# Layer 0's input projection in a two-layer encoder: three float32r passes in place of exact fp32 products, and another order in the last piece

## The chip, the core and the metric

The kernel runs on one core of one Trainium2 chip. The metric is the device time of one execution in microseconds; the time before is the median of three runs. Names of engines: PE (TensorE, the matrix engine), with its weight loads listed apart; DVE (VectorE); ACT (ScalarE); POOL (GpSimd); SP (SyncE, which issues the transfers). Results of matmuls are collected in PSUM, in eight banks of 128 x 512 fp32; six of them are "acc" tiles here and two serve everything else.

## What is computed

The reference is a trunk of two encoder layers on 256 positions of width 2048, in float32. Cut to what matters here:

```python
c_act = jax.nn.silu(c)
for l in range(2):
    mod = (c_act @ w_mod[l] + b_mod[l]).reshape(1, 6, 2048)
    shift_m, scale_m, gate_m, shift_f, scale_f, gate_f = ...
    h = layer_norm(x) * (1.0 + scale_m) + shift_m
    proj = h @ w_in[l]                       # 2048 x 4288
    uv, q_c, kv_c, k_r, sb, sc, sh, ag = jnp.split(proj, IN_SPLITS, axis=-1)
    y_a = gmlp_mixer(uv, ...)                # gelu, layer norm of v, mixing over positions
    y_b = mla_mixer(q_c, kv_c, k_r, ...)     # attention with latent q and kv
    y_c = sb * causal_dwconv(sc * sh, sconv_w[l])
    y_d = conformer_conv(ag, ...)            # a * sigmoid(g), conv of 31 taps, norm, silu
    y = concat([y_a, y_b, y_c, y_d]) @ w_out[l]
    x = layer_norm(ALPHA * x + (1.0 + gate_m) * y, ...)
    h = layer_norm(x) * (1.0 + scale_f) + shift_f
    x = layer_norm(ALPHA * x + (1.0 + gate_f) * conv_ffn(h, ...), ...)
```

Each weight is read once, some 600 MB in all.

## The kernel before

**Two ways to multiply.** A product of fp32 operands can be made exactly, as one matmul call on fp32 tiles (the trace shows it as two matmul records), or in three float32r passes: each operand is taken apart into a rounded high half and the remainder, and high x high, high x low and low x high are added in PSUM. The function `weights` (L420) loads a weight tile for either. With `exact` it loads straight into buffers of the pool `splitp` (tags whi and wlo, four tiles of 128 x 1024 each), which the products read as they are. Otherwise it loads into one of the four raw buffers of 128 x 2048 (`rawp`), ACT casts the high half into a whi tile (L455), and DVE subtracts it from the raw tile to get the low half, wlo (L456). `split` (L472) does the same to activations (L474, L475).

**Groups of columns.** The 4288 columns of w_in are handled as D (the GLU pair, 1024 columns), U and V (512 each, for the gMLP branch), E (512, the gate of the short convolution), B (q, kv and the rotary key: 704, read as 768) and C (1024). A unit of a group is `nk` k tiles of 128 rows. `group` (L477) makes such a group over all sixteen k tiles: `load(u)` calls `weights`, `products` issues the matmuls, `end` calls what follows. With `hF` given, all its units are exact. `stream` (L399) issues one unit: the load, the products of the unit before, `pump()` (which takes steps of the modulation stream at a rate set for each phase), and up to `bg` items from the list `background`.

**Layer 0 by pieces.** In layer 0 the normalised input must wait for shift and scale, which are themselves products with w_mod. So `by_pieces` (L1174) goes over the k tiles in five pieces of 2, 2, 4, 4 and 4 (`PIECES`), and while one piece is multiplied, the modulation columns of the next are made: `mod_piece` loads w_mod and DVE multiplies and adds it into `qacc` (L235), PE sums over partitions (`ps_mod`), and the next piece's activations are scaled and, from the fifth k tile on (`PLAIN_KT = 4`), split into halves in `hT`. Within a piece the D group comes in quarters, and U, V and E stand between them: D, U, D, V, D, E, D. `chan_major` issues the products of D, U and E (channels on partitions, 256 positions moving), and V is made with positions on partitions (512 channels moving). D adds up in four PSUM tiles through all pieces. U, V and E use two at a time; `side` adds each piece's result to a sum in SBUF. In the first two pieces all is exact. In the other three the D group passes in halves, while U, V and E are exact:

```python
for j, p in enumerate(weights(w_in, kt, nk, c0, width, exact or g != "D")):
```

`terms` returns one product or three, by whether the weight part has a low half.

**What follows.** After the last piece come `mix_d` (sigmoid and product of the GLU pair; it then puts the 4 x 31 taps of the convolution and `norm_d` into `background`, one item each; the first tap of each of four channel blocks runs on ACT, the other thirty on DVE, L834), `mix_u`, `gelu_v` and `mix_v` (the gMLP branch), then the B group with seven background items a unit and 1.3 modulation steps a unit, the C group with eight and 1.6 (`STEPS`, `RATES`), and the output projection in three column chunks, the first in halves and the other two exact. The modulation stream (`mod_stream`) makes the rows or columns of the remaining five modulations of layer 0 and of layer 1, sixteen loads of 1 MB and sixteen DVE steps into `macc` (L235) for each; the loads use the same four raw buffers. The second half of the positions of the last chunk of the output projection stands behind the sums of shift_f and scale_f (`before` in `out_proj`), which are among the first three modulations of the stream.

**Order.** The program text gives each instruction its place in a priority order; the engines' queues are then filled by a scheduler that takes what it holds to be ready, so the trace's order need not be that of the text. Each engine, and SP's queue of loads, executes its own instructions in order.

Of the kernel before, what the change touches and what calls it, by code (L numbers as in the profile page):

```python
# [14 lines left out]
D = 2048  # L15
# [3 lines left out]
KT = D // P  # L19
# [6 lines left out]
C_UV, C_Q, C_SB, C_SC, C_AG = 0, 1024, 1728, 2240, 3264  # L26
# [13 lines left out]
STEPS = [  # L40
    dict(B=7, C=8, up=2),
    dict(U=6, B=5, C=6, E=6, up=2),
]

PIECES = ((0, 2), (2, 2), (4, 4), (8, 4), (12, 4))

PLAIN_KT = 4


@with_exitstack  # L50
def encoder_kernel(ctx: ExitStack, tc: tile.TileContext, A: dict, consts: bass.AP, out: bass.AP):
# [337 lines left out]
    background = []  # L389
# [84 lines left out]
        act.copy(hi, src)  # L474
        dve.tensor_tensor(out=lo, in0=src, in1=hi.bitcast(F32), op=ALU.subtract)  # L475

    def group(w, c0, width, name, then, ntm=0, nk=2, hF=None, bg=0, spare=0):  # L477

        ncm = (width - 512 * ntm) // P
        box = {}

        def products(item, u):
            if u == 0:
                box["c"] = [acc_tile(f"{name}_c{i}") for i in range((ncm + 1) // 2)]
                box["t"] = [[acc_tile(f"{name}_t{t}{i}") for i in range(ntm)] for t in range(2)]
                box["h"] = list(hT)
            for part in (range(0, min(4, ncm)), range(4, ncm)):
                for k, (hi, lo) in enumerate(item):  # L490
                    kt = u * nk + k
                    st, sp = kt == 0, kt == KT - 1
                    for i in part:
                        o = box["c"][i // 2][:, (i % 2) * S : (i % 2 + 1) * S]
                        off = slice(i * P, (i + 1) * P)
                        first = st and i % 2 == 0
                        if lo is None:
                            mm(o, hi[:, off], hF(kt), first, sp)
                        else:
                            xh, xl = (h[:, kt % 2, :] for h in box["h"][kt // 2][:2])  # L500
                            mm(o, hi[:, off], xh, first, False)
                            mm(o, hi[:, off], xl, False, False)
                            mm(o, lo[:, off], xh, False, sp)
            for k, (hi, lo) in enumerate(item):
                kt = u * nk + k
                st, sp = kt == 0, kt == KT - 1
                for i in range(ntm):
                    off = slice(ncm * P + i * 512, ncm * P + (i + 1) * 512)
                    for t in range(2):
                        tok = slice(t * P, (t + 1) * P)  # L510
                        o = box["t"][t][i]
                        if lo is None:
                            mm(o, hF(kt)[:, tok], hi[:, off], st, sp)
                        else:
                            xh, xl = (h[:, kt % 2, tok] for h in box["h"][kt // 2][:2])
                            mm(o, xh, hi[:, off], st, False)
                            mm(o, xh, lo[:, off], False, False)
                            mm(o, xl, hi[:, off], False, sp)

        def load(u, spare=spare):  # L520
            return weights(w, u * nk, nk, c0, width, hF is not None, spare if u == 0 else 0)

        def end():
            then(box["c"], box["t"])

        return KT // nk, load, products, end, bg
# [52 lines left out]
    def run(g):  # L579
        units, load, products, end, bg = g  # L580
        for u in range(units):
            stream(lambda: load(u), lambda item, u=u: products(item, u), bg)
        pending.append(end)
# [590 lines left out]
    def by_pieces(l, w_in, hF, between, mix_d, mix_u, gelu_v, mix_v, mix_b, mix_c, mix_e):  # L1174
# [27 lines left out]
        def side(g, parts, k0, nkt):  # L1202
            ps = [acc_tile(f"{g}{l}_{i}") for i in range(2)]
            for kt, part in parts:
                st, sp = kt == k0, kt == k0 + nkt - 1
                if g == "V":
                    ts = terms(kt, part)
                    for t in range(2):
                        for n, (w, x) in enumerate(ts):
                            mm(ps[t], x[:, t * P : (t + 1) * P], w, st and n == 0, sp and n == len(ts) - 1)  # L1210
                else:
                    chan_major(ps, kt, part, range(4), st, sp)
            for i in range(2):
                if k0 == 0:
                    act.copy(sums[g][i], ps[i])
                elif k0 + nkt == KT:
                    dve.tensor_tensor(out=sums[g][i], in0=ps[i], in1=sums[g][i], op=ALU.add)
                else:
                    part = tmp_tile("part")
                    act.copy(part, ps[i])  # L1220
                    dve.tensor_tensor(out=sums[g][i], in0=part, in1=sums[g][i], op=ALU.add)
# [3 lines left out]
        for q, (k0, nkt) in enumerate(PIECES):  # L1225
            ahead = between(q + 1) if q + 1 < len(PIECES) else ([], None)
            exact = k0 < PLAIN_KT
            loaded = {}

            def load(g, kt):  # L1230

                c0, width = (C_AG, 1024) if g == "D" else (cols[g], 512)
                nk = min(2048 // width, nkt)
                for j, p in enumerate(weights(w_in, kt, nk, c0, width, exact or g != "D")):
                    loaded[(g, kt + j)] = p

            mods_left = list(ahead[0])
            units = len(mods_left)

            def some_mods(share):  # L1240
                while mods_left and (units - len(mods_left)) < units * share:
                    mods_left.pop(0)()

            def d_part(kt, half):
                if ("D", kt) not in loaded:
                    load("D", kt)
                chan_major(accD, kt, loaded[("D", kt)], range(4 * half, 4 * half + 4), kt == 0, kt == KT - 1)

            turns_d = [(kt, h) for kt in range(k0, k0 + nkt) for h in range(2)]
            n = len(turns_d) // 4  # L1250
            for s in range(4):
                mine = turns_d[s * n : (s + 1) * n]
                if ("D", mine[0][0]) not in loaded:
                    load("D", mine[0][0])
                some_mods((0.3, 0.7, 1.0, 1.0)[s])
                if s == 3 and ahead[1] is not None:
                    ahead[1]()
                for kt, h in mine:
                    d_part(kt, h)
                if s < 3:  # L1260
                    g = "UVE"[s]
                    load(g, k0)
                    some_mods((0.5, 0.85, 1.0)[s])
                    side(g, [(kt, loaded[(g, kt)]) for kt in range(k0, k0 + nkt)], k0, nkt)
        mix_d(accD, None)
        mix_u(sums["U"], None)
        for t in range(2):
            gelu_v(t, sums["V"][t])
        mix_v()
        phase(l, "B")  # L1270
        run(group(w_in, C_Q, 768, f"B{l}", mix_b, hF=hf, bg=STEPS[l]["B"]))
        phase(l, "C")

        def mix_ce(cps, tps):
# [260 lines left out]
```

## Time and profile before

| what | value |
|---|---|
| median of three runs | 2287.88 us (2284.08 to 2291.81) |
| the profiled execution, its own time | 2285.5 us |
| its span | 2283.7 us |
| mean granted PE clock | 0.991 |
| bytes moved | 605.21 MB, mean 265 GB/s |
| layer 0's input projection, first matmul to the end of C | 33 to 325 us |
| its five pieces end at about | 51, 79, 119, 155 and 190 us |

In a row of a view by groups stand the source line, engine, operation, the tiles written and read, their shapes and the count; then busy us and the mean ns of one; then the idle time of the engine just before, and what ended it. L79 is the helper that issues matmuls, so products are told apart by tile names: `hF` and `wexact` are exact operands, `whi`, `wlo` and `hT` are halves. In a row of the order of time stand the start, the length, and what ran, merged where equal instructions follow each other. A matmul's length there includes its way through the array, so rates are taken from starts. Stretches of the span are given as start:end in us from the span's start.

### The profile page before, as it was taken

What the parts mean: (1) busy time and instruction counts of PE and PEld (TensorE: products, weight loads), DVE (VectorE), ACT (ScalarE), POOL (GpSimd) and SP (SyncE); (2) the same over time, 40 slices, a digit from 0 to 9 for tenths busy, and PEclk for the clock granted to TensorE, in tenths of its full rate; (3) what the DMA queues carried; (4) which work ended last, traced back from release to release, by engine and by line L of the source; (5) the groups of instructions that cost most, each with busy time, mean ns of one, the idle gap of its engine ahead of it and who ended that gap; (6) DMA issues with size and microseconds to landing.
All of it is one profiled execution on the core that took longest, in us unless ns stands there. A gap on an engine that the chain in (4) does not pass through costs nothing. (4 is left out here: it accounts for less than half of the span.)

```text
span 2283.7 us, 30024 instructions
## 1 busy us (share of the span) xinstructions
PE 2226.7 (98%) x11682; PEld 1859.8 (81%) x11682; DVE 1788.8 (78%) x2270; ACT 1049.8 (46%) x1525; POOL 35.3 (2%) x59
## 2 busy tenths in 40 slices
PE   5899999999999999999999999999999999999998
PEld 4688886478888888887887999877888888888886
DVE  6878998598888898998976799787776565665676
ACT  2221141355554544544556434556555554454553
POOL 2000000000000000000000000000000000000000
PEclk9999999999999999999999999999999999999999
DMA  9999889778998988888974666876765556555554
GB/s 348 368 335 342 304 301 393 301 267 304 319 329 302 323 312 327 317 316 304 319 258 148 200 214 240 291 268 223 247 223 190 184 182 199 186 196 190 193 194 147
DMA packets 224566, 605.21 MB, mean 265 GB/s; under 512 B 14548, under 2 KB 27076, under 8 KB 202660
## 3 DMA queue, kind: packets, MB, share of 16 engines
q1 hardware_dynamic: 223576, 602.30, 74.7%
q8 instruction: 91, 1.49, 0.3%
q0 software_dynamic: 848, 1.01, 0.1%
q14 instruction: 51, 0.42, 0.0%
HBM read 601.16 MB, written 2.10 MB: 264 GB/s over the span
## 5 line engine op out<-in xcount | busy, mean ns | idle before, releaser
L456 DVE TENSOR_TENSOR wlo<-wraw,whi 128x1024 fp32r<-128x1024 f32 (+1 forms) x624 | 749.6, 1214 | 315.5 <-ACT whi L455 309.4
L455 ACT CAST whi<-wraw 128x1024 fp32r<-128x1024 f32 (+1 forms) x624 | 649.2, 1047 | 727.2 <-PE g_c L79 204.4
L79 PE MATMUL v_c<-hT,whi 128*128 128x512 f32 x1408 | 493.1, 394 | 0.0
L79 PE MATMUL g_c<-hT,whi 128*128 128x512 f32 x1280 | 448.2, 394 | 0.0
L79 PE MATMUL v_c<-hT,wlo 128*128 128x256 f32 x1408 | 394.3, 280 | 0.0
L79 PE MATMUL d<-whi,a 128*128 128x512 f32 x1344 | 387.9, 390 | 0.0
L235 DVE SCALAR_TENSOR_TENSOR macc<-wmod,cact,macc 128x2048 f32<-128x2048 f32 x150 | 351.6, 2344 | 17.1 <-DMA wmod<-in_w_mod_dram 16.8
L79 PE MATMUL g_c<-hT,wlo 128*128 128x256 f32 x1280 | 358.4, 280 | 0.0
L79 PEld LDWEIGHTS v_c<-hT,whi 128*128 128x128 f32 x1408 | 263.9, 187 | 61.0
L79 PEld LDWEIGHTS d<-whi,a 128*128 128x128 f32 x1344 | 252.9, 188 | 52.4
L79 PEld LDWEIGHTS g_c<-hT,whi 128*128 128x128 f32 x1280 | 239.9, 187 | 55.6
L79 PEld LDWEIGHTS v_c<-hT,wlo 128*128 128x128 f32 x1408 | 265.8, 189 | 0.2
L79 PEld LDWEIGHTS g_c<-hT,wlo 128*128 128x128 f32 x1280 | 241.7, 189 | 0.2
L79 PE MATMUL d<-wlo,a 128*128 128x512 f32 x672 | 233.8, 390 | 1.9 <-DVE wlo L456 1.9
L79 PEld LDWEIGHTS d<-wlo,a 128*128 128x128 f32 x672 | 126.6, 188 | 29.1 <-DVE wlo L456 2.7
L79 PE MATMUL o<-whi,a 128*128 128x512 f32 x352 | 102.3, 398 | 2.3 <-ACT whi L455 2.3
L834 DVE SCALAR_TENSOR_TENSOR convD<-gluD,pm,convD 128x237 f32<-128x237 f32 (+26 forms) x240 | 99.0, 458 | 0.5
L474 ACT CAST a<-g 128x512 fp32r<-128x512 f32 x132 | 81.1, 616 | 36.7 <-PE d L79 34.2
L79 PE MATMUL D_c<-hT,whi 128*128 128x256 f32 x448 | 85.7, 292 | 4.0 <-ACT hT L474 3.0
L475 DVE TENSOR_TENSOR a<-g,a 128x512 fp32r<-128x512 f32 x132 | 87.5, 683 | 1.8 <-ACT a L474 1.8
L566 PE MATMUL first<-wexact,hN 128*128 128x512 f32 x192 | 85.7, 596 | 1.5 <-ACT hN L82 1.2
L235 DVE SCALAR_TENSOR_TENSOR qacc<-wmod,cact,qacc 128x1024 f32<-128x1024 f32 (+1 forms) x75 | 80.2, 1070 | 2.4 <-DMA wmod<-in_w_mod_dram 0.4
(311 smaller groups left out, 2462.3 us busy)
## 6 DMA issues: line engine op xcount, KB each, us to landing
wraw<-in_ffn_w_up_dram SPq DMA_DIRECT2D x168, 1024.0 KB, 5.2
wmod<-in_w_mod_dram SPq DMA_DIRECT2D x160, 1024.0 KB, 6.6
wraw<-in_ffn_w_down_dram SPq DMA_DIRECT2D x88, 1024.0 KB, 5.3
wmod<-in_w_mod_dram SPq DMA_DIRECT2D x64, 512.0 KB, 7.9
wraw<-in_w_in_dram SPq DMA_DIRECT2D x30, 1024.0 KB, 5.5
wexact<-in_w_in_dram SPq DMA_DIRECT2D x52, 512.0 KB, 6.7
wraw<-in_w_out_dram SPq DMA_DIRECT2D x24, 1024.0 KB, 7.3
wexact<-in_w_out_dram SPq DMA_DIRECT2D x16, 512.0 KB, 11.0
```

The costliest lines, as they stand in the source:

```text
L79: pe.matmul(o, lhsT, rhs, start=start, stop=stop, skip_group_check=True)
L235: i = dve.scalar_tensor_tensor(out=acc, in0=w, scalar=col, in1=acc, op0=ALU.mult, op1=ALU.add)
L455: held(act.copy(hi[:, :m], r), "cast")
L456: i = dve.tensor_tensor(out=lo[:, :m], in0=r, in1=hi[:, :m].bitcast(F32), op=ALU.subtract)
L474: act.copy(hi, src)
L475: dve.tensor_tensor(out=lo, in0=src, in1=hi.bitcast(F32), op=ALU.subtract)
L566: i = pe.matmul(ps, hN[kt // 4][:, kt % 4, t * P : (t + 1) * P], parts[kt], start=kt == 0, stop=kt == KT - 1, skip_group_check=True,)
L834: dve.scalar_tensor_tensor(out=yd[:, j, 30 - k :], in0=glu[:, j, : S - 30 + k], scalar=CW(k, j), in1=yd[:, j, 30 - k :], op0=ALU.mult, op1 ...
```

## The change

Four edits, all in layer 0's input projection:

1. U, V and E of pieces 3, 4 and 5 pass in halves as D does: `exact` alone decides.
2. `group` gets a parameter `plain`, the number of first k tiles that stay exact where `hF` is given (all of them by default). The B group is called with `plain=PLAIN_KT`, so its units of k tiles 4 to 15 pass in halves. The C group isn't changed.
3. In the last piece all eight half-turns of D come first, then U, V and E. `mix_d` is called after the load of U, no longer after the loop.
4. After each of U, V and E in that piece, eight items of `background` (`TAPS_ASIDE`), which are taps of the convolution, are issued.

```diff
+TAPS_ASIDE = 8
...
-    def group(w, c0, width, name, then, ntm=0, nk=2, hF=None, bg=0, spare=0):
+    def group(w, c0, width, name, then, ntm=0, nk=2, hF=None, bg=0, spare=0, plain=KT):
...
         def load(u, spare=spare):
-            return weights(w, u * nk, nk, c0, width, hF is not None, spare if u == 0 else 0)
+            exact = hF is not None and u * nk < plain
+            return weights(w, u * nk, nk, c0, width, exact, spare if u == 0 else 0)
...
-                for j, p in enumerate(weights(w_in, kt, nk, c0, width, exact or g != "D")):
+                for j, p in enumerate(weights(w_in, kt, nk, c0, width, exact)):
                     loaded[(g, kt + j)] = p
...
             turns_d = [(kt, h) for kt in range(k0, k0 + nkt) for h in range(2)]
+            if k0 + nkt == KT:
+
+                for kt, h in turns_d:
+                    d_part(kt, h)
+                for g in "UVE":
+                    load(g, k0)
+                    if g == "U":
+                        mix_d(accD, None)
+                    side(g, [(kt, loaded[(g, kt)]) for kt in range(k0, k0 + nkt)], k0, nkt)
+                    for _ in range(TAPS_ASIDE):
+                        background.pop(0)()
+                continue
...
-        mix_d(accD, None)
         mix_u(sums["U"], None)
...
-        run(group(w_in, C_Q, 768, f"B{l}", mix_b, hF=hf, bg=STEPS[l]["B"]))
+        run(group(w_in, C_Q, 768, f"B{l}", mix_b, hF=hf, bg=STEPS[l]["B"], plain=PLAIN_KT))
```

## The prediction

> **What bounds the kernel now.** I read the page first (busy times, then the chain), then the busy times of seven stretches of layer 0, then the order of time of PE and VectorE there.
>
> ```profile
> span 2283.7 us, 30024 instructions
> PE 2226.7 (98%) x11682; PEld 1859.8 (81%) x11682; DVE 1788.8 (78%) x2270; ACT 1049.8 (46%) x1525; POOL 35.3 (2%) x59
> PE 32%; DVE 1%; ACT 0%; issue 0%; DVEq 0%; POOL 0%; POOLq 0%; ACTq 0%
> ```
>
> The chain of waits is PE, but it reaches back to the middle of the program only. The change lies in the first tenth, so that tenth is cut into stretches: pieces 3, 4 and 5 of the input projection, the q/kv group, the C group with the attention, the first and the other two column chunks of the output projection. After the name of the stretch come its length and the busy times of PE, weight loads, DVE, ACT and POOL, the granted clock, the DMA share and GB/s.
>
> ```profile
> 79.20:119.10 39.90, 34.97 (x178) 28.50 (x178) 33.24 (x36) 10.47 (x16) 0.00 (x0) 0.91 1.02 372
> 119.10:154.60 35.50, 34.76 (x194) 28.51 (x193) 30.29 (x34) 9.50 (x14) 0.00 (x0) 1.00 0.96 351
> 154.60:189.90 35.30, 35.30 (x204) 29.80 (x204) 18.73 (x20) 6.30 (x9) 0.00 (x0) 1.00 0.94 327
> 189.90:234.00 44.10, 44.10 (x218) 38.91 (x216) 42.65 (x83) 9.75 (x20) 2.83 (x5) 1.00 0.92 326
> 234.00:325.40 91.40, 91.28 (x436) 76.27 (x435) 84.83 (x141) 22.23 (x42) 3.69 (x2) 1.00 0.86 314
> 325.40:380.60 55.20, 52.09 (x227) 41.31 (x225) 49.71 (x45) 18.59 (x25) 0.00 (x0) 0.94 0.91 340
> 380.60:425.30 44.70, 44.70 (x104) 19.80 (x105) 31.48 (x26) 2.18 (x7) 0.00 (x0) 1.00 1.03 405
> ```
>
> From 119 us on PE has next to no gap, so work taken off PE there shortens the kernel if nothing else is late. But VectorE (DVE) is at 97% in the q/kv stretch (42.65 of 44.10) and 93% in the C stretch, and the transfers run at 0.86 to 1.03. Only piece 5 has much free VectorE time: 35.30 - 18.73 = 16.6 us. ScalarE is far from full.
>
> **What PE saves.** Start times of consecutive PE runs give the price of a pass. An exact fp32 product appears as two matmul records.
>
> ```profile
> 89.17 0.40 PE L79 MATMUL D_c<-hT,whi 128*128 128x256 f32 x2
> 89.42 0.28 PE L79 MATMUL D_c<-hT,wlo 128*128 128x256 f32 x1
> 89.53 0.40 PE L79 MATMUL D_c<-hT,whi 128*128 128x256 f32 x2
> 126.22 7.07 PE L79 MATMUL U<-hF,wexact 128*128 128x256 f32 x32
> 132.94 0.47 PE L79 MATMUL D_c<-hT,whi 128*128 128x256 f32 x1
> 135.16 7.03 PE L79 MATMUL V<-wexact,hF 128*128 128x512 f32 x16
> 142.28 1.10 PE L79 MATMUL D_c<-hT,whi 128*128 128x256 f32 x7
> 203.07 30.38 PE L79 MATMUL B_c<-hF,wexact 128*128 128x256 f32 x140
> 334.66 1.07 PE L79 MATMUL o<-whi,a 128*128 128x512 f32 x4
> 335.57 0.62 PE L79 MATMUL o<-wlo,a 128*128 128x512 f32 x2
> 336.02 1.07 PE L79 MATMUL o<-whi,a 128*128 128x512 f32 x4
> ```
>
> Three float32r passes of 256 columns take 89.53 - 89.17 = 0.36 us. The exact product of the same block takes (132.94 - 126.22)/16 = 0.42. So a U or E group of a piece of four k tiles (16 blocks) saves 0.96 us. V moves 512 columns: exact (142.28 - 135.16)/8 = 0.89, less a little wait at its end, so about 0.87; three passes, from six in 1.36 us, take 0.68; eight of them save 1.5. A piece saves 0.96 + 1.5 + 0.96 = 3.4 us. The q/kv group has six blocks in each k tile; its k tiles 4 to 15 give 72 blocks x 0.06 = 4.3. Its first two units and the whole C group stay exact. In all: 3 x 3.4 + 4.3 = 14.5 us.
>
> The Trainium skill (TensorE: Matmul & The Clock Gate, back-to-back issue gap) puts a lone warm pass of N columns at N/2.4 + 2.5 ns, 109 ns for 256. By that, three passes would be an estimated 0.33 us and the saving half as large again; the row's 0.12 per pass decides, since it holds the weight load as well.
>
> **What it adds.** Each weight tile that passes in halves costs a cast on ScalarE and a subtraction on VectorE. Rows by group, of the stretch from piece 5 to the end of the q/kv group (VectorE) and of piece 4 (ScalarE): count, then busy us and mean ns of one, then the idle time before.
>
> ```profile
> L834 DVE SCALAR_TENSOR_TENSOR convD<-gluD,pm,convD 128x255 f32<-128x255 f32 (+29 forms) x58 | 22.9, 461 | 0.0
> L235 DVE SCALAR_TENSOR_TENSOR macc<-wmod,cact,macc 128x2048 f32<-128x2048 f32 x9 | 21.1, 2348 | 6.2 <-DMA wmod<-in_w_mod_dram 6.2
> L456 DVE TENSOR_TENSOR wlo<-wraw,whi 128x1024 fp32r<-128x1024 f32 x2 | 2.4, 1220 | 4.5 <-ACT whi L455 4.5
> L475 DVE TENSOR_TENSOR hT<-hF,hT 128x512 fp32r<-128x512 f32 x2 | 1.3, 688 | 0.9 <-ACT hT L474 0.9
> L455 ACT CAST whi<-wraw 128x1024 fp32r<-128x1024 f32 x4 | 4.1, 1044 | 12.3 <-DMA wraw<-in_w_in_dram 12.3
> ```
>
> A piece gets six subtractions of 128x1024: 6 x 1.22 = 7.2 us. The six later units of the q/kv group get twelve of 128x768, between 0.69 (512 columns) and 1.22 (1024), so about 0.95: 11 us. ScalarE gets 18 casts x 1.04 and 12 of some 0.85, 29 us in stretches where it is 20 to 30% busy: nothing, unless a cast is late. The activations need no new split, since the halves are made for the D group already. The bytes are the same, with fewer issues on SP's queue (one of 1 MB for two of 512 KB); but they now land in the four raw buffers that the modulation columns use, no longer in the eight split buffers.
>
> The 24 taps cost VectorE 23 x 0.39 = 9 us (22.9/58; one tap of 31 is ScalarE's), moved from the C group into piece 5. GLU first adds no work: the sigmoid and two products of mix_d move from the end of piece 5 to its middle.
>
> **Pieces 3 and 4: nothing gained.** The next piece waits for its modulation columns, which are VectorE's longest queue.
>
> ```profile
> 134.56 7.88 DVE L235 SCALAR_TENSOR_TENSOR qacc<-wmod,cact,qacc 128x1024 f32<-128x1024 f32 x6
> 145.83 2.60 DVE L235 SCALAR_TENSOR_TENSOR qacc<-wmod,cact,qacc 128x1024 f32<-128x1024 f32 x2
> 153.16 1.84 PE L79 MATMUL ps_mod<-ones,qacc 128*128 128x1 f32 x16
> ```
>
> In piece 4 the last column step ends at 148.4, and PE comes to its sum at 153.2, after E. With 7.2 us of subtractions ahead of it, less some 2 us of VectorE waits that these fill, that step ends at 153.6: PE's 3.4 us become idle time. VectorE would need 30.29 + 7.2 = 37.5 of 35.5 us, but what lies behind the last step can slip. I take +0.5 for both pieces; the bounds are -1 (VectorE's waits in piece 3, 6.7 us, take all) and +5 (nothing slips: 2 for piece 4, 0.5 for piece 3, and as much again where loads wait for raw buffers).
>
> **Piece 5 and the q/kv group: 3.4 + 4.3 = 7.7 us off PE.** What can eat it is VectorE. Carried from stretch to stretch: piece 5 needs 18.73 + 7.2 + 9 = 35 of a stretch of 32, so 3 to 4 us move on. The q/kv stretch needs 42.65 + 11 + 4 = 58 of 40; 18 move on. The C stretch gives up 9 of taps: 84.8 + 18 - 9 = 94 of 91; at the 97% that the q/kv stretch shows, 5 move on. The first output chunk then has 55 of 55, and passes on some 3. So VectorE is full for 225 us; all depends on what it leaves late. Taps and modulation steps can be late; a weight half can't, for PE stands behind it.
>
> I price the waits for halves in the q/kv group at 4 us (bounds 0, when each half overtakes the taps, and 13, the rival below), in piece 5 at 1 (the first halves of U; 0 to 3), and behind the C group at 2.5 (0 to 8), for this reason:
>
> ```profile
> 414.99 2.34 DVE L235 SCALAR_TENSOR_TENSOR macc<-wmod,cact,macc 128x2048 f32<-128x2048 f32 x1
> 425.31 3.71 PE L79 MATMUL ps_mod<-ones,macc 128*128 128x1 f32 x32
> ```
>
> The second half of the output projection waits, on PE, for this sum. Its last step ends at 417.3; PE arrives at 425.3, 8 us later. If PE gains 7.7 the two meet; every us by which the steps are later than today then costs one, and the transfers cannot hurry them (1.03, 405 GB/s).
>
> **A wait costs more than its length.** Stretches behind a PE wait of 3.03 us (83.0) and of 2.27 us (372.8), same columns:
>
> ```profile
> 83.00:87.20 4.20, 4.08 (x18) 3.92 (x19) 4.17 (x6) 0.58 (x2) 0.00 (x0) 0.50 0.83 273
> 372.80:377.60 4.80, 4.68 (x12) 3.48 (x13) 4.62 (x3) 0.95 (x1) 0.00 (x0) 0.64 1.00 422
> ```
>
> The granted clock was 0.50 and 0.64, so 4.2 x 0.50 = 2.1 and 4.8 x 0.36 = 1.7 us more were lost. Of the 4 us in the q/kv group I count two as such a loss. The Trainium skill (TensorE: Matmul & The Clock Gate, HAM oscillation) warns of gaps over about 3.4 us; here 2.3 were enough. By its threshold the short waits would be free of this, and the 4 would be 2.
>
> **The sum**, against the profiled execution (2285.5 us, a span of 2283.7 and 1.8 around it): 2285.5 + 0.5 - 7.7 + 1 + 4 + 2.5 = 2285.8. That execution lies 2.4 below the median of the three runs; I add half of this: 2287.
>
> **Rivals.** (A) The halves always overtake taps and steps, and the steps end no later. For it, VectorE's order of time in the C stretch, where halves stand between single taps:
>
> ```profile
> 303.63 1.22 DVE L456 TENSOR_TENSOR wlo<-wraw,whi 128x1024 fp32r<-128x1024 f32 x1
> 304.76 0.94 DVE L834 SCALAR_TENSOR_TENSOR convD<-gluD,pm,convD 128x229 f32<-128x229 f32 x2
> 305.62 1.22 DVE L456 TENSOR_TENSOR wlo<-wraw,whi 128x1024 fp32r<-128x1024 f32 x1
> ```
>
> Against it: 225 us without slack. 2285.5 - 7.7 = 2278.
>
> (B) Slower: VectorE serves taps and steps in the order in which they are written, so each half of the q/kv group stands behind the earlier unit's seven taps and 1.3 steps. To the end of that group VectorE has 18.73 + 42.65 + 7.2 + 11 + 9 = 88.6 us, less 5 behind the last half, so that half is ready at 154.6 + 83.6 = 238.2, and PE's last unit (12 x 0.36 = 4.3) ends at 242.5, not 233.3: +9.2. It decides from the third unit on, the first in halves; the C stretch can't give it back, as PE is full there (91.28 of 91.40). With one loss of clock of 2 us: 2285.5 + 11.2 = 2297. For it: VectorE's 97%. Against it: the C stretch again.
>
> (C) Slower: the raw buffers. The queue that issues loads waits for them already; waits from 80 to 430 us, total, times, longest:
>
> ```profile
> SPq L346 <- DVE macc L235: 55.6, 20, 5.6
> SPq L346 <- DVE wlo L456: 28.2, 7, 8.2
> SPq L441 <- DVE qacc L235: 6.7, 5, 2.2
> ```
>
> Piece 3 and 4 then ask for 13 buffers instead of 10 each, the q/kv group for 16 instead of 10, and each load stands behind a modulation load which stands behind VectorE. One longest wait (5.6) in each of pieces 3 and 4, of which the 3.4 saved there absorb part (2.2 left each), and one in the q/kv group: 2285.8 + 4.4 + 5.6 = 2296.
>
> (D) The change doesn't do what it says: instructions aren't issued in the order written. This modulation step is written with the q/kv group, whose PE work begins at 189.9, and it ran inside piece 5:
>
> ```profile
> 170.05 1.29 DVE L233 TENSOR_SCALAR macc<-wmod,cact 128x2048 f32<-128x2048 f32 x1 [0.91 <-DMA wmod<-in_w_mod_dram]
> ```
>
> So the taps need not lie beside U, V, E. Then 9 us stay behind in the q/kv and C stretches, half of it before a half: 2285.8 + 4.5 = 2290.
>
> **Chances.** Forecast 0.42 (its own range 2281 to 2293), A 0.20, B 0.20, C 0.13, D 0.05. A measurement of this kernel tells about 0.3%, 6.9 us, from no change: faster is below 2281.0, slower above 2294.7. A gives nearly all of faster, B and C nearly all of slower, and the forecast's ends a little of both: 0.20, 0.45, 0.35. The range goes from 2277 (A, with 1 us of pieces 3 and 4) to 2302 (B or C with 5 us more, such as the upper bound of pieces 3 and 4).
>
> **What would show it.** Right: float32r matmuls of U, E and B_c at 0.12 us from start to start; pieces 3 and 4 as long as now with PE idle before the sum of the columns; piece 5 some 3 us shorter, VectorE near 95% in it, with taps; the q/kv group near 40 us with PE waits for wlo of a few us; the last macc step nearer to its sum than 8 us. Wrong: PE waits for wlo or whi of over 8 us in the q/kv group (B), SP's waits on raw buffers grown and the transfer share down in pieces 3 and 4 (C), or none of these and the sum of the last steps met at 418 (A). A change behind 450 us would be wrong for every case here.

## The result and the profile after

The changed kernel takes 2312.17 us (median of four runs, 2308.08 to 2315.19) beside 2288.44 for the kernel before: a ratio of 1.0104, 95% interval 1.0078 to 1.0129, or 24 us slower. The forecast was 2287, and its range ended at 2302.

First the page of the changed kernel, the busy times:

```profile
span 2312.7 us, 30465 instructions
PE 2228.4 (96%) x11874; PEld 1875.4 (81%) x11874; DVE 1819.3 (79%) x2300; ACT 1077.7 (47%) x1555; POOL 33.6 (1%) x59
```

The span grew by 29.0 us in this execution, while VectorE's busy time grew by 30.5 (1819.3 - 1788.8), near the 33 us of subtractions. The stretches of the changed kernel that answer to the seven of the prediction follow, in the same columns. Their borders are the sums behind pieces 2, 3 and 4, the last product of piece 5, the first sum behind the q/kv group, the first product of the output projection, a cut in time at 405, and the second sum of the finished modulations; the prediction's borders lie up to 1.5 us behind these events.

```profile
81.50:122.30 40.80, 30.91 (x180) 28.06 (x179) 34.61 (x36) 15.65 (x20) 0.00 (x0) 0.79 0.89 320
122.30:163.30 41.00, 34.07 (x235) 31.28 (x234) 36.94 (x38) 15.90 (x21) 0.00 (x0) 0.92 0.94 333
163.30:200.10 36.80, 36.80 (x289) 35.84 (x288) 30.15 (x41) 21.28 (x29) 0.00 (x0) 1.00 0.77 247
200.10:259.60 59.50, 48.12 (x297) 44.81 (x296) 59.36 (x99) 11.61 (x19) 2.84 (x5) 0.89 0.75 256
259.60:348.50 88.90, 88.90 (x431) 74.80 (x429) 78.33 (x127) 25.27 (x49) 1.86 (x2) 1.00 0.86 322
348.50:405.00 56.50, 51.61 (x217) 40.32 (x216) 48.18 (x42) 15.85 (x20) 0.00 (x0) 0.91 0.86 331
405.00:452.50 47.50, 45.78 (x111) 20.61 (x110) 34.92 (x29) 0.00 (x0) 0.00 (x0) 1.00 1.03 405
```

The fourth row is the result: from the last product of piece 5 to the end of the q/kv group 59.5 us pass. VectorE is busy for 59.36 of them, PE for 48.12, at a mean clock of 0.89. Each run has one profiled execution. Measured between the same events in PE's order of time, the stages of all runs are these (us; "start" is the time of the sum behind piece 2, and the last two columns go from the first product of the output projection to the first and from there to the second sum of the finished modulations):

```
                         start   p3    p4    p5   q/kv   C    to 1st  to 2nd
before                    78.1  39.5  35.5  36.5  43.6  92.1  28.0    72.0
after                     81.5  40.8  41.0  36.8  59.5  88.9  34.4    69.6
e1  q/kv exact            79.3  39.2  41.3  36.8  43.5  93.3  29.5    70.2
e2  order alone           79.2  40.0  35.5  39.6  43.5  95.4  28.5    71.6
e3  q/kv halves + order   79.6  41.6  35.5  41.0  50.0  89.8  34.4    70.2
e4  no taps in q/kv       80.3  40.7  40.9  36.8  49.1  91.9  35.6    71.5
e5  loads apart           78.8  41.7  42.9  41.5  54.8  88.9  28.8    70.2
e6  no steps in q/kv      78.7  39.1  40.7  36.8  39.1  96.0  45.0    72.1
e7  halves in p5 alone    80.0  41.6  35.5  37.3  43.7  93.3  31.9    69.5
e8  exact from raw        78.8  44.7  37.8  36.7  44.1  94.0  28.5    71.4
e9  no subtraction        78.4  38.5  40.5  36.8  45.4  91.9  28.5    70.8
e10 extra work, exact     78.8  40.1  35.5  36.5  45.2  88.9  46.5    63.8
e11 some put off          79.1  41.2  41.0  36.8  38.5  91.0  43.9    76.1
e12 q/kv alone, put off   78.6  40.1  35.5  36.5  38.3  89.8  56.4    70.7
e13 apart, no subtraction 78.5  40.4  35.6  36.4  39.4  92.0  28.8    70.6
e14 GpSimd                78.2  41.6  44.6  36.8  81.7  93.8  33.2    71.2
e15 apart, GpSimd         78.5  46.9  43.3  39.1  69.9  91.8  28.5    72.5
```

So of 29 us, 15.9 arise in the q/kv stage, 5.5 in piece 4, 1.3 in piece 3, 6.4 in the first output chunk; C and the last column give back 5.6; 0.3 lie in piece 5 and 1.8 behind the second sum. The 3.4 us before piece 3 lie ahead of the pieces that were edited; the other runs are at 78.2 to 80.3, among them some with the same pieces 3 (e1, e6, e11: 78.7 to 79.3), so that is scatter of this execution. The borders between pieces depend on PE's order: the E group of piece 4 runs ahead of its sum before the change and behind it (to 171.3) after it, so it counts with piece 5 there. Each edit also changes the order that the scheduler makes of the rest: in the changed kernel, e3, e5 and e10 some products of the C group run inside the q/kv stage, in the others none.

What PE and the casts wait for in that stage, from the waits of the changed kernel between 200.1 and 259.6 us (engine and what waited, releaser: total, times, longest):

```profile
ACT whi L457 <- DMA wraw<-in_w_in_dram: 30.5, 5, 12.2
...
PE B_c L81 <- DVE wlo L458: 9.1, 4, 4.3
...
PE C_c L81 <- DMA wexact<-in_w_in_dram: 2.3, 1, 2.3
```

And what SP's queue waits for there before it can issue a load:

```profile
SPq L348 <- DVE mixed L940: 16.9, 1, 16.9
SPq L348 <- DVE wlo L458: 13.7, 4, 5.3
SPq L443 <- DVE convD L838: 10.3, 4, 2.6
```

PE waits for low halves (9.1 us). Two things lie behind that. One is VectorE's queue; here is ScalarE's first cast for this group, then VectorE's order of time ahead of PE's longest wait, which ends at 217.68:

```profile
198.80 0.83 ACT L457 CAST whi<-wraw 128x768 fp32r<-128x768 f32 x1 [0.77 <-DMA wraw<-in_w_in_dram]
```

```profile
207.71 2.00 DVE L838 SCALAR_TENSOR_TENSOR convD<-gluD,pm,convD 128x239 f32<-128x239 f32 x5
...
214.03 2.73 DVE L838 SCALAR_TENSOR_TENSOR convD<-gluD,pm,convD 128x231 f32<-128x231 f32 x7
216.67 0.95 DVE L458 TENSOR_TENSOR wlo<-wraw,whi 128x768 fp32r<-128x768 f32 x1
217.54 0.45 DVE L838 SCALAR_TENSOR_TENSOR convD<-gluD,pm,convD 128x227 f32<-128x227 f32 x1
217.91 0.95 DVE L458 TENSOR_TENSOR wlo<-wraw,whi 128x768 fp32r<-128x768 f32 x1
```

Casts and subtractions of the group follow in the same order, so the first subtraction belongs to the first cast: made at 198.80, yet subtracted at 216.67, behind taps and steps of the gMLP branch. At the other three waits, too, the cast was done before VectorE came to the half. The other is the loads: SP issued nothing between 195.87 and 213.21, since the next modulation load waited 16.9 us for the raw buffer that holds the gMLP weights, and the loads of halves stood behind it. That is why ScalarE waited 12.2 us for the load of its fifth cast, at 226.99; the longest wait of PE was over by then.

What filled VectorE's queue, from its groups of that stage before (189.7 to 233.3 us) and after:

```profile
L834 DVE SCALAR_TENSOR_TENSOR convD<-gluD,pm,convD 128x255 f32<-128x255 f32 (+29 forms) x57 | 22.5, 461 | 0.0
L235 DVE SCALAR_TENSOR_TENSOR macc<-wmod,cact,macc 128x2048 f32<-128x2048 f32 x6 | 14.1, 2345 | 2.1 <-DMA wmod<-in_w_mod_dram 2.1
```

```profile
L838 DVE SCALAR_TENSOR_TENSOR convD<-gluD,pm,convD 128x246 f32<-128x246 f32 (+29 forms) x63 | 26.6, 462 | 0.0
L237 DVE SCALAR_TENSOR_TENSOR macc<-wmod,cact,macc 128x2048 f32<-128x2048 f32 x8 | 18.8, 2344 | 0.0
L458 DVE TENSOR_TENSOR wlo<-wraw,whi 128x768 fp32r<-128x768 f32 x12 | 11.3, 950 | 0.0
```

The halves were added, and no tap or step left the stage for them: in its longer time it holds 63 taps and 8 steps, where it held 57 and 6 before.

A wait again costs more than its length. In PE's order of time:

```profile
217.68 0.58 PE L81 MATMUL B_c<-hT,wlo 128*128 128x256 f32 x1 [4.30 <-DVE wlo L458]
...
220.19 0.63 PE L81 MATMUL B_c<-hT,whi 128*128 128x256 f32 x2
220.62 0.41 PE L81 MATMUL B_c<-hT,wlo 128*128 128x256 f32 x1
220.83 0.63 PE L81 MATMUL B_c<-hT,whi 128*128 128x256 f32 x2
...
251.51 4.34 PE L81 MATMUL C_c<-hF,wexact 128*128 128x256 f32 x12 [2.25 <-DMA wexact<-in_w_in_dram]
```

Three passes take 220.83 - 220.19 = 0.64 us here, not 0.36: more than the exact product's 0.42. The window's row (bounds, length, then busy us and instructions of PE, PEld, VectorE, ScalarE, GpSimd, granted clock, DMA share, GB/s) shows why:

```profile
217.70:222.00 4.30, 4.30 (x20) 4.30 (x21) 4.30 (x6) 0.00 (x0) 0.00 (x0) 0.50 0.50 141
```

PE is busy throughout, at half the clock; that lasts to 223.8.

With this the stage adds up. PE's own work is 43.6 - 4.3 = 39.3 us. It stands idle for 59.50 - 48.12 = 11.4, of which 9.1 are the waits for low halves and 2.3 one for a load of the C group. The clock takes 0.11 x 59.5 = 6.5. The twelve records of C products in the last row, which PE ran while the last halves of the group were late, are 2.5 at 0.21 each. That makes 59.7 of 59.5 us, and it is also why the C stage is shorter afterwards.

### The profile page after: what moved, and what is told of

The parts are those of the page before. It is cut to its first block, busy times and chain, and to the rows that moved or that the text cites. A ratio compares the mean times of both kernels' runs of the same rounds, so it can differ in the third digit from the quotient of the medians.

```text
span 2312.7 us, 30465 instructions
## 1 busy us (share of the span) xinstructions
PE 2228.4 (96%) x11874; PEld 1875.4 (81%) x11874; DVE 1819.3 (79%) x2300; ACT 1077.7 (47%) x1555; POOL 33.6 (1%) x59
## 3 DMA queue, kind: packets, MB, share of 16 engines
q0 software_dynamic: 848, 1.01, 0.1%
## 5 line engine op out<-in xcount | busy, mean ns | idle before, releaser
L457 ACT CAST whi<-wraw 128x1024 fp32r<-128x1024 f32 (+1 forms) x654 | 676.8, 1043 | 761.0 <-PE g_c L81 202.9
L458 DVE TENSOR_TENSOR wlo<-wraw,whi 128x1024 fp32r<-128x1024 f32 (+1 forms) x654 | 782.7, 1210 | 311.6 <-ACT whi L457 305.5
L838 DVE SCALAR_TENSOR_TENSOR convD<-gluD,pm,convD 128x251 f32<-128x251 f32 (+25 forms) x240 | 101.7, 461 | 0.4
L81 PEld LDWEIGHTS o<-whi,a 128*128 128x128 f32 x352 | 67.5, 193 | 18.3 <-ACT whi L457 3.9
```

The source lines that it names most:

```text
L81: pe.matmul(o, lhsT, rhs, start=start, stop=stop, skip_group_check=True)
L457: held(act.copy(hi[:, :m], r), "cast")
L458: i = dve.tensor_tensor(out=lo[:, :m], in0=r, in1=hi[:, :m].bitcast(F32), op=ALU.subtract)
L838: dve.scalar_tensor_tensor(out=yd[:, j, 30 - k :], in0=glu[:, j, : S - 30 + k], scalar=CW(k, j), in1=yd[:, j, 30 - k :], op0=ALU.mult, op1 ...
```

## The experiments

Two theories were set against each other. **V**: VectorE's added work, and with it the place of the halves in its queue. **B**: the loads, which now land in the four raw buffers behind modulation loads. The T and R of two expectations ask only in which stage the loss arises. Comparisons are with the kernel before, run on the same chip; the ratios weigh all runs and differ by up to 0.0014 from the quotients of the medians.

### One part of the change at a time

**e1**, the q/kv group exact again:

```diff
-        run(group(w_in, C_Q, 768, f"B{l}", mix_b, hF=hf, bg=STEPS[l]["B"], plain=PLAIN_KT))
+        run(group(w_in, C_Q, 768, f"B{l}", mix_b, hF=hf, bg=STEPS[l]["B"]))
```

> As the changed kernel, but the q/kv group exact again. Theory T (the loss of 16 us between the end of piece 5 and the end of the q/kv group is made by the halves of that group): that stage falls from 59.7 us to 44 to 47, and the kernel to about 2296, the 8 us left being pieces 3 and 4. Rival R (VectorE's work and the loads are late already when the q/kv group begins, and the halves there only show it): the stage stays over 52 us, the kernel over 2303.

Measured 2294.75, ratio 1.0016 (1.0003 to 1.0028), q/kv stage 43.5 us. The q/kv halves make the loss of that stage. Piece 4 keeps its 41.3.

**e2**, the order alone: e1, and U, V, E exact (`exact or g != "D"`).

> As the changed kernel, but with U, V, E and the q/kv group exact: only the GLU group first and the 24 taps beside U, V, E remain. If the order is free and the taps use VectorE's idle time of piece 5: 2284 to 2290. If the order itself costs (U, V, E in one row without D's quarters between them, their sums and loads bunched): 2293 or more.

Measured 2290.04, ratio 1.0007 (0.9995 to 1.0020): no difference at the end. The order isn't free on the way, though: in its execution piece 5 and the C stage are 3.1 and 3.3 us longer, and the second sum comes 8.1 us later than before. 5.4 of these come back in the feed-forward of layer 0, from the first product of `v_c` to the first of `d`: 471.5 us instead of 476.9, with PE busy throughout and at full clock in both. Eight of the seventeen executions are near the shorter figure (471.4 to 473.0), nine near the longer (476.7 to 477.7); why isn't settled. So a difference of 5 us can arise far behind the change. Stages are compared up to the second sum only; if the difference goes with the kernel and not with the execution, small ratios hold it too.

**e3**, the q/kv group in halves with the new order, U, V, E exact:

```diff
-                for j, p in enumerate(weights(w_in, kt, nk, c0, width, exact)):
+                for j, p in enumerate(weights(w_in, kt, nk, c0, width, exact or g != "D")):
```

> As the changed kernel, but U, V, E exact in all pieces; the q/kv group in halves, the order kept. Theory T: the stage from the end of piece 5 to the end of the q/kv group stays at 54 us or more, the kernel at 2298 to 2304. Rival R: with nothing late from the pieces the stage falls to 40 to 46 us and the kernel is at 2284 to 2291.

Measured 2301.53, ratio 1.0056 (1.0039 to 1.0073), stage 50.0: the time is as T said, the stage between the two. The q/kv halves cost 11 us over e2 (1.0056 - 1.0007), U, V, E alone 2 (e1 over e2), and both together 22 (1.0104 - 1.0007). Together they cost more than the sum. That fits their drawing on the same VectorE time (in e3 piece 5 has no halves of its own), but no run shows it by itself.

**e7**, halves in piece 5 alone (U, V, E of pieces 3 and 4 and the q/kv group exact):

```diff
-                for j, p in enumerate(weights(w_in, kt, nk, c0, width, exact)):
+                for j, p in enumerate(weights(w_in, kt, nk, c0, width, exact or (g != "D" and k0 + nkt < KT))):
```

> As the changed kernel, but U, V, E of pieces 3 and 4 and the q/kv group exact: halves in piece 5 alone, with the order and the taps. If piece 5 has the room that the prediction gave it (35 us of VectorE work in 32 to 35): its PE saving of 3.4 us comes through, 2283 to 2287 beside 2290 for the order alone. If not: 2290 or more.

Measured 2296.39, ratio 1.0041 (1.0024 to 1.0057): the second case, PE's saving doesn't come through. Piece 5 is 2.3 us shorter than in e2, but the first output chunk is 3.4 longer. At the second sum e7 is even 0.6 us ahead of e2 (432.8, 433.4), so what it loses more than e2 arises behind the stages of the table. Why it costs 9 us in all isn't settled.

### What stands in VectorE's queue

**e4**, no taps written with the q/kv group:

```diff
-    dict(B=7, C=8, up=2),
+    dict(B=0, C=13, up=2),
```

> As the changed kernel, but no taps are written with the q/kv group's units; the C group takes thirteen a unit instead of eight. Theory V (the low halves stand in VectorE's queue behind the taps): some 50 taps x 0.39 = 20 us leave the stage, it falls from 59.7 us to 42 to 46, the kernel to 2298 to 2302. Rival B (the loads come late, since the four raw buffers are held by modulation steps and by the gMLP weights): the stage stays at 53 us or more, the kernel at 2307 or more.

Measured 2304.21, ratio 1.0069 (1.0052 to 1.0086). The stage falls by 10.4 us to 49.1; V had said 14 to 18. The edit takes fewer taps out of the stage than the 50 expected: the scheduler still puts 32 there, 31 fewer than in the changed kernel, which is 12 us at 0.39. C and the first chunk give 4 back.

**e6**, no modulation steps written with the q/kv group:

```diff
-    dict(B=1.3, C=1.6, out=2.1, up=0.7, down=0.7),
+    dict(B=0.0, C=2.9, out=2.1, up=0.7, down=0.7),
```

> As the changed kernel, but no modulation step is written with the q/kv group (rate 0 instead of 1.3 a unit); the C group takes 2.9 a unit instead of 1.6. Theory B: the loads of halves have nothing in front of them but the gMLP weights, the q/kv stage falls to 42 to 48 us. Theory V gives the same for it, 8 steps x 2.34 = 19 us less, 42 to 46 us. Both: what is put off comes back behind the C group, where the sums of the next modulation are waited for: +5 to +12 there; the kernel 2300 to 2308. Were the stage over 52 us, both would be wrong and the taps alone to blame.

Measured 2313.77, ratio 1.0119 (1.0097 to 1.0140), over the 2300 to 2308 expected. Its q/kv stage, C stage and the way to the first sum:

```profile
195.30:234.40 39.10, 38.96 (x285) 37.10 (x284) 39.04 (x86) 11.46 (x19) 1.84 (x4) 1.00 0.50 155
234.40:330.40 96.00, 92.12 (x442) 77.18 (x440) 85.92 (x128) 24.17 (x52) 2.86 (x2) 1.00 0.91 347
330.40:375.50 45.10, 32.53 (x122) 24.31 (x122) 42.78 (x36) 11.20 (x13) 0.00 (x0) 0.85 0.90 339
```

The stage is 20.4 us shorter than in the changed kernel, near the eight steps (18.8) that are gone from it, and as short as PE alone would make it (39.3). All of it comes back: 7 us in C, 11 in the output chunk and 2.5 to the second sum. In the output chunk PE is busy for 32.53 of 45.10 us.

**e11** and **e12** put off less. e11 is e4 with rates `B=0.6, C=2.0, out=2.4`. e12 is the kernel before with the q/kv group in halves (`plain=PLAIN_KT`), `B=3, C=12` taps and rates `B=0.9, C=1.8, out=2.3`.

> As the changed kernel, with no taps and 0.6 instead of 1.3 modulation steps a unit in the q/kv group; the C group takes thirteen taps and 2.0 steps a unit, the first two output chunks 2.4 steps a unit instead of 2.1. Theory V: the q/kv stage at 39 to 42 us; the C stage and what follows give back 5 to 10; the kernel 2296 to 2303, between no taps alone (2304) and the kernel with the q/kv group exact (2295). Over 2306: what is put off costs in full.

> As the kernel before (order, exact U, V, E), with the q/kv group in halves, three taps and 0.9 steps a unit there instead of 7 and 1.3, and twelve taps and 1.8 steps in the C group, 2.3 steps in the first two output chunks. Theory V: piece 5's idle VectorE time takes steps early as before, the q/kv stage is at 39 to 42 us (4 less than exact); if nothing comes back later 2284 to 2286, if it does 2288 to 2296.

Measured 2304.20, ratio 1.0073 (1.0048 to 1.0098), and 2303.64, ratio 1.0071 (1.0054 to 1.0087): the first a little over what was expected, the second 8 us over. Their q/kv stages are 38.5 and 38.3 us, 5 less than before, and the way to the first sum is 43.9 and 56.4 instead of 28.0. No order tried removes the loss; it moves.

**e10**, VectorE work that nothing waits for, in the kernel before:

```diff
         def load(u, spare=spare):
+            if name == "B0":
+                for _ in range(2):
+                    dve.tensor_tensor(out=tmp_tile("extra"), in0=X[0][:, 0:512], in1=X[1][:, 0:512], op=ALU.subtract)
```

> As the kernel before, but sixteen VectorE subtractions of 128x512 (16 x 0.69 = 11 us, as much as the halves of the q/kv group) are written with the exact q/kv group, and nothing waits for them. If the mere amount of VectorE work sets the time: +8 us or more, 2296 or more. If what counts is that PE waits for a half that stands in VectorE's queue: the q/kv stage stays at 43.6 +-1 and the kernel at 2286 to 2293.

The group of that line from 150 to 260 us (out<-in, partitions x elements, count | busy, mean ns | idle before):

```profile
L523 DVE TENSOR_TENSOR extra<-x,x 128x512 f32<-128x512 f32 x16 | 10.8, 680 | 0.0
```

Measured 2294.85, ratio 1.0042 (1.0022 to 1.0062): 9.6 us (0.0042 x 2288; 5 to 14 by the interval) for 10.8 us of work, though the q/kv stage is 45.2, only 1.6 longer. At the second sum its execution is 10.1 us behind. PE's order of time behind the C group, products of `norm_d` and of the output projection:

```profile
333.03 2.16 PE L79 MATMUL ps_var<-ones,sqD 128*128 128x1 f32 x16 [1.27 <-ACT sqD L864]
338.80 1.22 PE L79 MATMUL ps_rD<-dgD,ones 128*128 128x256 f32 x2 [3.61 <-DVE dgD L879]
...
350.55 0.73 PE L79 MATMUL o<-wlo,a 128*128 128x512 f32 x2 [3.15 <-DVE wlo L456]
```

The taps end later, the norm behind them stands within the output projection, and PE waits for it and for the halves of w_out. So VectorE work costs time here even where nothing waits for its result: at this place and in this order, the kernel before had little usable room between the pieces and the output projection.

### Loads and subtractions, taken away

**e5**, halves land in activation slots instead of the raw buffers:

```diff
+        if land:
...
+                r = slot("land")
+                nc.sync.dma_start(out=r[:, :m].rearrange("p (k c) -> p k c", k=per), in_=...)
+                hi = splitp.tile([P, 1024], F32R, tag="whi", name="whi")
+                lo = splitp.tile([P, 1024], F32R, tag="wlo", name="wlo")
+                act.copy(hi[:, :m], r[:, :m])
+                dve.tensor_tensor(out=lo[:, :m], in0=r[:, :m], in1=hi[:, :m].bitcast(F32), op=ALU.subtract)
...
```

> As the changed kernel, with the same casts and subtractions, but the weights of U, V, E and of the q/kv group land in free activation slots and no longer in the four raw buffers. Theory B (raw buffers: loads of weights stand in one queue behind modulation loads that wait for VectorE): pieces 3 and 4 return to 38 to 40 and 35 to 37 us, the q/kv stage falls from 59.7 us to 45 to 50, the kernel to 2290 to 2298. Theory V (VectorE's work alone): no stage changes by more than 2 us, the kernel stays at 2308 to 2314.

Measured 2306.94, ratio 1.0092 (1.0070 to 1.0115), stage 54.8, pieces 3 and 4 at 41.7 and 42.9: B alone falls. With VectorE's work in place the loads are worth some 3 us (0.0012 x 2288; 6 by the medians), which is less than the two intervals are wide. PE still waits 6.5 us for low halves in its q/kv stage.

**e8**, e2 with U, V, E landing in the raw buffers, multiplied exactly from there:

```diff
+        if exact == "raw":
+            raw = raw_tile("wraw")
...
+            return [(raw[:, k * width : (k + 1) * width], None) for k in range(nk)]
...
-weights(w_in, kt, nk, c0, width, exact or g != "D")
+weights(w_in, kt, nk, c0, width, exact or ("raw" if g != "D" else False))
```

> As the kernel with the order alone (all of U, V, E exact), but U, V, E of pieces 3 to 5 land in the raw buffers, as they do in the changed kernel, and are multiplied from there: no cast, no subtraction. Theory B: piece 4 is 3 to 6 us longer than with the order alone (35.5 us), since the modulation loads share four buffers with them. Theory V: pieces 3 and 4 stay within 1.5 us of 40.0 and 35.5.

Measured 2296.81, ratio 1.0036 (1.0021 to 1.0050): pieces 3 and 4 are 4.7 and 2.3 us longer than in e2 with no more VectorE work. Sharing the buffers has a price of its own.

**e9**, the third pass uses the high half again and no subtraction is made, so the result lacks these low halves:

```diff
             held(act.copy(hi[:, :m], r), "cast")
+            if nolo:
+                for j in range(per):
+                    parts.append((hi[:, j * width : (j + 1) * width], hi[:, j * width : (j + 1) * width]))
+                continue
```

> As the changed kernel, with the same loads, casts and three passes, but without the subtractions on VectorE in U, V, E and the q/kv group: the third pass uses the high half again, so the low half of these weights is left out of the result. Theory V (VectorE's 33 us): the q/kv stage is at 39 to 42 us, piece 4 at 34 to 37, and the kernel shows the PE saving, 2278 to 2287. Rival B (raw buffers and loads): the q/kv stage stays over 50, piece 3 over 43, the kernel over 2300.

Measured 2293.14, ratio 1.0026 (1.0015 to 1.0038): without VectorE's work the loss is 6 us, not 24, between what the two theories said. V is the larger part, yet PE's saving doesn't show. What waits now, from the waits of that kernel between 117 and 240 us, which hold piece 4 and the q/kv group:

```profile
ACT whi L457 <- DMA wraw<-in_w_in_dram: 35.1, 8, 6.4
...
PE V L81 <- ACT whi L457: 6.2, 1, 6.2
...
PE B_c L81 <- ACT whi L457: 4.9, 2, 2.5
```

PE waits for casts, and the casts for loads.

**e13**, e9 and e5 together:

> As the changed kernel, without the subtractions of U, V, E and the q/kv group (their low halves are left out, the high half passes again in their place) and with these weights landing in activation slots instead of the raw buffers: both suspected causes taken away together. Theory V+B (VectorE's work makes three quarters of the loss, late loads the rest): the waits of V for its cast go, piece 4 falls from 40.5 to 32 to 36 us, the q/kv stage from 45.4 to 39 to 41, and the kernel to 2276 to 2284, where PE's saving shows. If it stays at 2290 or more, a third cause is left.

Measured 2283.11, ratio 0.9977 (0.9961 to 0.9993), 5 us faster than before, though with an incomplete result as in e9. Its piece 4 and q/kv stage:

```profile
118.90:154.50 35.60, 31.60 (x236) 29.46 (x234) 30.38 (x32) 15.90 (x21) 0.00 (x0) 1.00 1.01 371
190.90:230.30 39.40, 38.29 (x282) 36.52 (x281) 39.33 (x67) 12.02 (x20) 2.53 (x4) 1.00 0.92 312
```

The q/kv stage is 4.2 us shorter than before, as PE's saving of 4.3 says. Piece 4 isn't: 35.6 us with PE busy for 31.6, VectorE for 30.4 and the transfers at 1.01. So the two causes together make the whole loss, and pieces 3 and 4 have nothing to give even then. Nor does piece 5: 36.4 us beside 36.5, with PE waiting 2.5 us there for halves of the activations. One thing isn't parted from V in e9 and e13: without subtractions more of the wlo tiles stay free for exact loads.

### The subtractions on GpSimd

**e14** is the changed kernel, **e15** the kernel of e5, each with `pool.tensor_tensor` for these 30 subtractions.

> As the changed kernel, but GpSimd does the 30 subtractions of U, V, E and the q/kv group; the result is complete. If VectorE's work is the cause and GpSimd is fast enough (under 3 us for 128x1024) and doesn't slow VectorE: about as without subtractions, 2290 to 2297. If GpSimd is slower than that or slows VectorE's instructions: 2305 or more.

> As the one before, with the weights landing in activation slots as well: a complete kernel with both causes taken away, if GpSimd is fast enough. 2278 to 2286 then, faster than before and after; 2300 or more if GpSimd is the new wait.

Measured 2343.05, ratio 1.0254 (1.0229 to 1.0279), and 2323.22, ratio 1.0163 (1.0143 to 1.0183). Groups of e14 from 80 to 280 us, GpSimd's by shape and one of VectorE's:

```profile
L458 POOL TENSOR_TENSOR wlo<-wraw,whi 128x1024 fp32r<-128x1024 f32 x18 | 49.7, 2774 | 84.3 <-ACT whi L457 84.3
L458 POOL TENSOR_TENSOR wlo<-wraw,whi 128x768 fp32r<-128x768 f32 x12 | 45.9, 3838 | 31.2 <-ACT whi L457 28.6 <-PE B_c L81 2.5
```

```profile
L237 DVE SCALAR_TENSOR_TENSOR qacc<-wmod,cact,qacc 128x1024 f32<-128x1024 f32 x30 | 51.4, 1714 | 4.1 <-DMA wmod<-in_w_mod_dram 3.3
```

GpSimd needs 2.77 us on average for 128x1024, which is within the 3 us asked for, but 3.84 for the smaller 128x768, and VectorE's steps of 128x1024 grow from 1.28 to 1.71 us on average. This way out is closed. No kernel of this study that computes the whole result is faster than the kernel before.

## Why the prediction was wrong

- **The step that failed is the account of the q/kv group**: "all depends on what it leaves late", priced at 4 us of waits for halves. It saw 18 us of VectorE work too much for that stage and let them move on as taps and steps. They didn't move on: the stage held more of both than before (63 taps and 8 steps, 57 and 6 before), they ran ahead of halves, and VectorE was busy for 59.36 of 59.5 us. PE waited 9.1 us for halves and lost 6.5 to the clock. The stage took 59.5 us where the sum had 43.3 (43.6 - 4.3 + 4).
- **Under it lies a second error**: that VectorE's idle time could be used. The account filled piece 5 to the last us and counted the C stretch and the output chunk as room. e10 shows that there was little: 10.8 us that nothing waits for cost 9.6. e6, e11 and e12 show the same from the other side: what leaves the q/kv stage returns behind the C group.
- **What PE saves: right in size where it shows.** Three passes take 0.36 us, and e13's q/kv stage is 4.2 us shorter (39.4 beside 43.6). Of the other 10 us, in pieces 3 to 5, no run shows a gain at the end.
- **What it adds: right.** The subtractions of 128x768 took 0.95 us, as estimated. VectorE's work from piece 5 to the end of the q/kv group is 30.15 + 59.36 = 89.5 us, where rival B had counted 88.6. That they lie so close is in part chance: fewer taps ran in piece 5 and more steps in the group than counted, and the borders differ by some us.
- **Pieces 3 and 4: "nothing gained" was right, +0.5 was not.** Measured +1.3 and +5.5, together beyond the bound of +5, and that without the E group of piece 4, which now counts with piece 5. The reason given, VectorE's queue of column steps, wasn't the only one: with its added work away and loads apart (e13) PE still gained nothing there, with the transfers at 1.01. And the cost wasn't that what lies behind the last step slips: the weights of V came late, from VectorE (e5) or from the raw buffers (e8, e9), and the clock fell (0.79 and 0.92).
- **Piece 5: not borne out.** 36.8 us between the events beside 36.5, where 2.4 less were forecast; part of that is the E group of piece 4, and PE was busy throughout. VectorE was busy for 30.15 of 36.80 us there, 82% and not 95. In e13, where halves cost VectorE nothing, the stage is no shorter either.
- **Behind the C group: +2.5 forecast, +2.6 measured (-3.2 + 6.4 - 2.4 + 1.8), by luck.** The loss arose ahead of the first sum and not at the second, where the prediction had put it.
- **Rival B was the mechanism of that stage**, at 0.20 instead of the largest chance, and its price of 9.2 + 2 was too low. It began at 154.6 with VectorE never idle. In fact piece 4 ended 10 us later, 6.6 us of piece 5 stayed idle, and the low clock came more than once. Its point that C can't give the loss back holds: C took 3.2 us less, 2.5 of which it had run inside the q/kv stage, and the output chunk 6.4 more.
- **Rival C** is the smaller part: 3 us with VectorE's work in place (e5), 11 without it (from 1.0026 to 0.9977 between e9 and e13).
- **Rival A** needed halves to overtake the taps. The rows quoted for it came from a stretch with two halves in 10 us; in the q/kv group a tap ran before nearly every half.
- **Rival D** was right in part: nine taps ran in piece 5, from 185.85 on, where 23 were counted, and the rest of the 23 fell to the stages behind. In e2, with exact weights, 25 ran there, and e2 shows that this alone is worth nothing.
- **A wait costs more than its length**: right, the clock was 0.50 for 6 us after the wait of 4.30 us. The Trainium skill's gap of about 3.4 us (TensorE: Matmul & The Clock Gate, HAM oscillation) agrees for this one. After the shorter wait of 2.88 us, which ended at 243.20, the clock was 0.50 from 244.3 to 247.7 all the same, as after the two short waits that the prediction shows.

## What to carry to other kernels

Before trading an engine's time for another's, add up the second engine over the whole stretch to the next point where everything waits, and ask which of its idle us can be reached: those spent waiting for a chain, or ahead of work that isn't ready, can't. A cheap test is to put in extra work of the same length that nothing waits for; if that costs nearly its length, expect the trade to be lost; here no order tried saved it. Moving the load between stages then shows as a shorter stage and a longer one behind it, so judge by the end and not by the stage.

## What the runs showed of the hardware beyond that

What GpSimd's subtraction took depended on what VectorE did meanwhile (in e14; the profile is rough on GpSimd). Two rows of GpSimd's order of time:

```profile
179.52 2.41 POOL L458 TENSOR_TENSOR wlo<-wraw,whi 128x1024 fp32r<-128x1024 f32 x1 [0.47 <-ACT whi L457]
...
223.63 12.32 POOL L458 TENSOR_TENSOR wlo<-wraw,whi 128x768 fp32r<-128x768 f32 x1 [5.33 <-ACT whi L457]
```

At 179.52 VectorE stood idle, and 128x1024 took 2.41 us, twice VectorE's 1.22. At 223.63 VectorE ran modulation steps and taps back to back, and the smaller 128x768 took 12.32 us, where one beside a nearly idle VectorE took 1.81 (at 216.50). VectorE was held up as well: its steps of 128x1024 took 1.71 us instead of 1.28 on average, while those of 128x2048 kept their 2.34. The Trainium skill (GPSIMD Engine Reference, Key points) says that GpSimd shares its SBUF interfaces with VectorE instructions that have two SBUF inputs. The same section calls VectorE about twice as fast in elementwise work. The trace agrees with both: the factor is 2.0 where VectorE was idle, and the longer times stand beside steps and taps, which read two tiles.
